# Slots for the recurrent unit's gates at the write, longer planned latencies, and down-product weights prepared one step ahead

## The chip, the core and the metric

The kernel runs on one core of a Trainium2 chip. The core's engines are TensorE (PE, with its weight loads as PEld), VectorE (DVE), ScalarE (ACT), GpSimd (POOL) and the queue of SyncE (SP), which issues most DMAs here. The metric is the device time of one execution in microseconds (us), as the median of several runs.

## What is computed

One decoder layer over 512 tokens of width 1024, in float32. All weight products are done as three passes of a split operand (high part times high part, high times low, low times high), so every weight tile has to be split into two tiles before its product.

```
proj = x @ w_in                                   # q k v z, b a, lru_x lru_g, gate_dn gate_lru
o    = gated_delta_rule(l2norm(silu(conv(q,k,v))), g, beta)   # 8 heads, scan over chunks
y_dn = (rmsnorm(o) * silu(z)) @ w_branch_dn
u    = conv(lru_x) + b
r, i = sigmoid(u @ w_a + b_a), sigmoid(u @ w_i + b_i)         # 10 blocks of 128
a    = exp(-8 r softplus(-lambda));  h = scan(a, sqrt(1 - a^2) * i * u)
y_lru = (h * gelu(lru_g)) @ w_branch_lru
h1   = layer_norm(alpha * x + (sig(g_dn) * y_dn + sig(g_lru) * y_lru) @ w_out)
out  = layer_norm(alpha * h1 + (silu(h1 @ w_gate) * (h1 @ w_up)) @ w_down)
```

## The kernel before

**Order of the work.** PE's instructions run in the order in which the program emits them. The other engines' instructions are put in order at compile time by a scheduler that goes by priority (program order, lifted inside `urgent()`) and by its own model of when data is ready; so an instruction late in the program can be placed long before its place there, if its data is ready and its engine has nothing earlier to do.

**First half (to about 500 us).** A planner writes PE's order. `before_merge` goes through the jobs of `ORDER` (k, q, v, z projections, l = a pair of recurrent blocks, g = merge gates) and takes the first whose number of free slots in `NEED` is there; each job is two columns of 8 steps, and `play` fetches columns two ahead. A step of a projection adds 0.68 to the planner's `clock`. Beside them run *chains*, generators that emit a few small matmuls, then yield how long PE was used and a planned latency from the table `LAT`; a chain is taken up again when the planner's clock has passed its due time. `dn_chain(p)` is the delta rule for two heads (p = 0 to 3): transposes and norms (`kt`), `kk`, a 16-step substitution on DVE (`sub`), block inverse steps `m1`, `m2`, `i1` to `i5`, then for four chunks `xr` (LAT `su`), `su` (LAT `ks`), `ks` (LAT `xr`), at last `oa`, `ob` and, 26 later, `ot`. `until(f"s{p-1}")` lets chain p begin its substitution only when chain p-1 is past `m2`. If no job fits, the planner adds 0.68 to its clock and goes on with the chains alone.

**Slots.** 40 SBUF slots of 128 x 1024 float32 are handed out in the order in which they came free. `slot()` takes one when the program text reaches it, `free()` gives it back; `room(n)` lets a chain wait, in planner time, for n free slots. `lru_pair(p)` takes three at its start (u, r, ig), though r and ig are first written in `lru_chain`, and `lru_chain` takes a and gl after its matmuls; the gelu that writes gl waits in planner time for that (`while p not in gls`).

**Feed-forward and down product.** After `play(ffn())` the down product is done as seven products q = 0 to 6 (a11, s1, s2, a12, s4, s3, a22), each in six steps m (five of two blocks of 256 rows, one of one). The sums s1 to s4 and the combined weights `td` make seven products of eight. A step loads its weights (`load_w`, three buffers), splits them with an ACT copy for the high part and a DVE subtract for the low part (`split_w`, three buffers each), and runs 12 matmuls of 512 columns. In the last product ("final") steps 3 to 5 have slots of their own and are run in one go, first for row block 2, then for row block 3. Results are added to the rows by `Norm.add` on DVE; `p7_done` does two such adds for each of row blocks 2 and 3 after s3. `Norm.finish` normalises: for row blocks 0 and 1 with ACT and four POOL instructions each, for 2 and 3 on DVE.

```
        for m, (p, n) in enumerate(blocks):
            keep = final and m >= 3
            extra = [flat(slot(f"wd{m}{e}", F32R)) if keep else None for e in range(2)]
            pend.append((m, n, *split_w(load_w(right(p, n)), None, *extra)))
            if not final:
                ready.append(left(products[q + 1][0], p, n))
```

So a step's weights are emitted right before its matmuls, and behind the adds of the step before. The last product's first accumulator `dl0` is the next bank of ring p, which is the one that s3 accumulated in for row block 2.

Of the kernel before, what the change touches and what calls it, by code (L numbers as in the profile page):

```python
# [9 lines left out]
F32R = mybir.dt.float32r  # L10
I32 = mybir.dt.int32
AF = mybir.ActivationFunctionType
# [8 lines left out]
         "z1 l3 v3 q3 g0 z2 g1 l4 g2 g3 z3 g4 g5 g6 g7")  # L21

LAT = {
    "F": 13.0, "kt": 12.0, "q": 5.2, "qk": 5.0, "P": 4.0, "vt": 2.0, "u": 10.0, "sub": 33.0, "m1": 7.0,
    "m2": 8.0, "i2": 6.0, "i4": 7.0, "i5": 7.0, "x": 8.0, "ks": 5.0, "xr": 7.0, "su": 6.5, "ot": 26.0,
    "ba": 9.0, "g": 2.5, "conv": 14.0,
}

# [5 lines left out]
P = 128  # L34
# [12 lines left out]
def layer_kernel(  # L47
# [23 lines left out]
    def slot(name, dt=F32):  # L71
        if not line:
            raise RuntimeError(f"no slot for {name}")
        tag = line.pop(0)
        t = big.tile([P, 2, T], dt, tag=tag, name=name)
        held[id(t)] = (t, tag)
        return t
# [12 lines left out]
    def bankp(name):  # L90
        return bank("p", name)

    def bankd(name):
        return bank("d", name)
# [19 lines left out]
    def flat(t):  # L114
        return t.rearrange("p a b -> p (a b)")
# [10 lines left out]
    def act(o, i, func, **kw):  # L126
        return S.activation(out=o, in_=i, func=func, **kw)  # L127
# [36 lines left out]
    def load_w(src, raw=None):  # L164

        wcount[0] += 1
        if raw is None:
            raw = wp.tile([P, 1024], F32, tag="wr", bufs=3, name=f"wr{wcount[0]}")
        v = view_w(raw, *src.shape[1:])
        nc.sync.dma_start(out=v, in_=src)  # L170
        return v

    def split_w(raw, eng=None, hi=None, lo=None):

        wcount[0] += 1
        if hi is None:
            hi = wp.tile([P, 1024], F32R, tag="wh", name=f"wh{wcount[0]}")
        if lo is None:
            lo = wp.tile([P, 1024], F32R, tag="wl", name=f"wl{wcount[0]}")
        n = raw.shape[1] * raw.shape[2]  # L180
        split_flat(hi[:, :n], lo[:, :n], raw.rearrange("p a b -> p (a b)"), eng)
        return view_w(hi, *raw.shape[1:]), view_w(lo, *raw.shape[1:])
# [80 lines left out]
    with tc.manual_schedule(engines={mybir.EngineType.Activation, mybir.EngineType.DVE}):  # L263
        for k in range(NK):
            transpose_x(k)
            if k == 1:
                n = NK * 16
# [20 lines left out]
    clock = [0.0]  # L288

    def advance(flush=False):  # L290
        while flush and chains:
            clock[0] += 0.68
            advance()
        for ch in list(chains):
            while ch in chains and ch[0] <= clock[0]:
                try:
                    pe, lat = next(ch[1])
                    ch[0] = clock[0] + pe + lat
                    clock[0] += pe
                except StopIteration:  # L300
                    chains.remove(ch)
# [19 lines left out]
    def start(gen, lat):  # L321
        chains.append([clock[0] + lat, gen])
# [113 lines left out]
    def room(n):  # L436
        while len(line) < n:
            assert clock[0] < 2000.0
            yield 0.0, 0.65
# [327 lines left out]
        yield 0.9, 0.0  # L767


    hs, gls = [None] * 5, {}  # L770

    def lru_pair(p):
        n0 = 2 * p
        u, r, ig = slot(f"u{p}"), slot(f"r{p}"), slot(f"ig{p}")
        gw = wg.tile([P, 4, P], F32, tag="gr" if p % 2 else "gs", name=f"gr{p}")
        nc.sync.dma_start(out=gw[:, 0:2], in_=lru_w_a[0, n0:n0 + 2].rearrange("n i o -> i n o"))
        nc.sync.dma_start(out=gw[:, 2:4], in_=lru_w_i[0, n0:n0 + 2].rearrange("n i o -> i n o"))

        def then_u(j, ps):
            conv(u[:, j], ps, lru_w, n0 + j, bias=lru_p(0, n0 + j))  # L780
            if j == 1:
                start(lru_chain(p, u, r, ig, gw), LAT["u"])

        keep = []

        def then_g(j, ps):
            keep.append(ps)
            if j == 1:
                while p not in gls:
                    clock[0] += 0.68  # L790
                    advance()
                with urgent():
                    for i in range(2):
                        act(gls[p][:, i], keep[i], AF.Gelu_apprx_tanh)
                done[f"gl{p}"] = clock[0]

        c = CLX + 256 * p
        yield from columns(win[:, :, c:c + 256], xT, f"lx{p}", then_u, G)
        c = CLG + 256 * p
        yield from columns(win[:, :, c:c + 256], xT, f"lg{p}", then_g, G)  # L800

    def lru_chain(p, u, r, ig, gw):
        n0 = 2 * p
        for g, (t, b) in enumerate(((r, 1), (ig, 2))):
            for j in range(2):
                ps = bankd(f"lw{p}_{g}_{j}")
                PE.matmul(ps, gw[:, 2 * g + j], u[:, j], start=True, stop=True)
                act(t[:, j], ps, AF.Sigmoid, bias=lru_p(b, n0 + j))
                if g == 0 or j == 0:
                    yield 0.86, PIECE  # L810
        if p == 0:
            lru_rates()
        a, gl = slot(f"a{p}"), slot(f"gl{p}")
        gls[p] = gl
        tt(V, u, u, ig, ALU.mult)
        m = ig
        for j in range(2):
            act(a[:, j], r[:, j], AF.Exp, scale=c8n[:, n0 + j:n0 + j + 1])
            act(r[:, j], r[:, j], AF.Tanh, scale=c8[:, n0 + j:n0 + j + 1])
        act(m, a, AF.Square)  # L820
        stt(m, m, 1.0, r, ALU.add, ALU.mult)
        act(m, m, AF.Sqrt, bias=tiny)
        V.memset(m[:, :, 0:1], 1.0)
        tt(V, m, m, u, ALU.mult)
        yield 0.86, 0.0
        yield from until(f"gl{p}")
        h = u
        for j in range(2):
            V.tensor_tensor_scan(out=h[:, j], data0=a[:, j], data1=m[:, j], initial=0.0,
                                 op0=ALU.mult, op1=ALU.add)  # L830
        tt(V, h, h, gl, ALU.mult)
        free(r, a, gl, ig)
        hs[p] = h
# [37 lines left out]
    for n in range(4 * NK):  # L871

        k, i = (n // 4, n % 4) if n < 24 else (6 + n % 2, (n - 24) // 2)
# [151 lines left out]
    for i in range(4):  # L1025
        t = slot(f"h1{i}")
# [49 lines left out]
    wgt, wup, wd = rows(w_ffn_gate[0]), rows(w_ffn_up[0]), rows(w_ffn_down[0])  # L1076
    NP = NF // 2
    parts = {n: [] for n in ("a12", "a22", "s1", "s2", "s3", "s4")}
    a11 = []
# [94 lines left out]
    def left(n, p, m):  # L1174

        t = slot(f"{n}{p}", F32R)
        split(t[:, 0, 0:256 * m], t[:, 1, 0:256 * m], flat(parts[n][p // 4])[:, 256 * (p % 4):256 * (p % 4 + m)])
        if p % 4 == 2 or p + m == NP:
            free(parts[n][p // 4])
        return t  # L1180
# [20 lines left out]
        ("s3", combined(1), ca, False, p7_done),  # L1201
        ("a22", combined(2), [], True, None),
    ]
    ready = a11
    for q, (name, right, banks, new, then) in enumerate(products):
        lhs, ready = ready, []
        final = q == 6
        tops = [[(0, b)] for b in banks]
        if final:

            tops = [[(0, bankp("dl0"))], [(0, bankd("dl1")[:, 0:256]), (256, bankd("dl2")[:, 0:256])]]
        pend = []
        for m, (p, n) in enumerate(blocks):
            keep = final and m >= 3
            extra = [flat(slot(f"wd{m}{e}", F32R)) if keep else None for e in range(2)]
            pend.append((m, n, *split_w(load_w(right(p, n)), None, *extra)))
            if not final:
                ready.append(left(products[q + 1][0], p, n))
            if keep and m < 5:
                continue  # L1220
            last = m == len(blocks) - 1
            for i in range(2):
                for c, ps in tops[i]:
                    w = ps.shape[1]
                    for mm, nn, wh, wl in pend:
                        for k in range(nn):
                            ts = slice(256 * k + P * i, 256 * k + P * i + P)
                            mm3(ps, lhs[mm][:, 0, ts], lhs[mm][:, 1, ts], wh[:, k, c:c + w], wl[:, k, c:c + w],
                                new and mm == k == 0, last and mm == m and k == nn - 1,
                                **({} if new else dict(skip_group_check=True)))  # L1230
                    if last:
                        if final:
                            lns[2 + i].add(ps, c, 1.0)
                        else:
                            then(i, ps)
                if last and (final or name == "s4"):
                    t = i if name == "s4" else 2 + i
                    lns[t].finish(final)
                    for jj in range(2):
                        (nc.sync if final else G).dma_start(out=out[0, t * P:(t + 1) * P, T * jj:T * jj + T],  # L1240
                                                            in_=h1[t][:, jj])
            pend = []
        free(*lhs)
# [24 lines left out]
```

## Time and profile before

| what | us |
|---|---|
| median of 3 runs | 1019.58 (1019.29 to 1020.12) |
| profiled execution, its own time | 1017.21 |
| its span, first to last instruction | 1015.5 |
| PE busy | 985.5 (97%) |
| DVE busy | 621.8 (61%) |
| ACT busy | 451.3 (44%) |
| POOL busy | 268.7 (26%) |
| mean granted TensorE clock | 0.995 |

The busy shares are means over stages of different kinds, and PE does the same matmuls whatever waits it meets: what an edit of order can give is read from PE's idle time, stage by stage. A PE row of the timeline gives in brackets the idle time just before it and what ended it. The clock column is the granted TensorE clock as a share of full speed.

### The profile page before, as it was taken

To read this page: it belongs to the slowest core of one execution; us is meant where nothing else is said; L and a number is where in the kernel's file an instruction comes from. 1 tells how busy PE (TensorE), PEld (TensorE's weight loads), DVE (VectorE), ACT (ScalarE), POOL (GpSimd) and SP (SyncE) were. 2 spreads that over 40 slices of the span, in tenths; PEclk is the share of its full clock that TensorE was granted. 3 is DMA by queue.
4 is the path that set the end of the run, shared out by engine and by line. 5 is a ranking of instruction groups with operands and counts; after the bars stand their busy time and mean duration, and the time that the engine had idled before them with its cause. 6 is when DMAs were issued, how large, how long until landed. Compare 5 with 4: busy or idle time off the path is not lost.

```text
span 1015.5 us, 14361 instructions
## 1 busy us (share of the span) xinstructions
PE 985.5 (97%) x5531; PEld 810.5 (80%) x5531; DVE 621.8 (61%) x1318; ACT 451.3 (44%) x619; POOL 268.7 (26%) x278
## 2 busy tenths in 40 slices
PE   7999999999999999999999999999999999999986
PEld 4887767777887888788888888798888888888875
DVE  3678999846777791265223464976344443388676
ACT  4598365359416743574322234322222222375451
POOL 2473534425343724265200003132000100000041
PEclk9999999999999999999999999999999999999998
DMA  8331322323222223234332527579354563346653
GB/s 255 105 104 53 84 74 63 84 73 84 64 63 73 75 66 89 63 112 127 103 94 84 171 88 207 187 268 327 110 163 154 181 207 90 97 136 195 194 188 107
DMA packets 161288, 128.52 MB, mean 127 GB/s; under 512 B 5499, under 2 KB 140860, under 8 KB 161220
## 3 DMA queue, kind: packets, MB, share of 16 engines
q1 hardware_dynamic: 152032, 99.12, 33.3%
q0 software_dynamic: 7872, 28.32, 7.5%
q8 instruction: 43, 0.70, 0.3%
q10 hardware_dynamic: 1316, 0.16, 0.1%
q14 instruction: 25, 0.20, 0.1%
HBM read 113.94 MB, written 13.65 MB: 126 GB/s over the span
## 4 chain that ended last, share of the span: by engine, by line
PE 75%; DVE 14%; ACT 4%; POOL 2%; issue 2%; DMA 1%; ACTq 0%; DVEq 0%; POOLq 0%
PE fu L157 4%; PE fg L157 4%; PE fg L155 4%; PE fu L155 4%; PE fu L156 4%; PE fg L156 4%; PE pj L155 3%; PE pj L156 3%; PE pj L157 3%; PE g L155 3%; PE g L157 3%; PE g L156 3%; DVE xa L121 3%; PE yl L157 2%; PE yl L156 2%
## 5 line engine op out<-in xcount | busy, mean ns | idle before, releaser
L135 ACT CAST wh<-wr 128x1024 fp32r<-128x1024 f32 (+1 forms) x163 | 168.5, 1034 | 363.2 <-PE fg L156 74.3
L121 POOL TENSOR_TENSOR wl<-wr,wh 128x512 fp32r<-128x512 f32 x128 | 172.4, 1369 | 216.0 <-ACT wh L135 211.5
L121 DVE TENSOR_TENSOR wl<-wr,wh 128x1024 fp32r<-128x1024 f32 x99 | 120.1, 1215 | 113.0 <-ACT wh L135 112.9
L155 PE MATMUL pj<-xT,wh 128*128 128x512 f32 x224 | 91.9, 410 | 0.0
L157 PE MATMUL pj<-xT,wl 128*128 128x512 f32 x224 | 87.5, 391 | 0.0
L156 PE MATMUL pj<-xT,wh 128*128 128x512 f32 x224 | 87.4, 390 | 0.0
L127 ACT ACT_TABLE_LOAD x62 | 79.5, 1283 | 12.4 <-DMA rw<-in_lru_conv_w 6.9
L155 PE MATMUL fg<-hk,wh 128*128 128x512 f32 x160 | 62.3, 389 | 0.0
L156 PE MATMUL fg<-hk,wh 128*128 128x512 f32 x160 | 62.3, 389 | 0.0
L157 PE MATMUL fg<-hk,wl 128*128 128x512 f32 x160 | 62.2, 389 | 0.0
L155 PE MATMUL fu<-hk,wh 128*128 128x512 f32 x160 | 62.2, 389 | 0.0
L156 PE MATMUL fu<-hk,wh 128*128 128x512 f32 x160 | 62.2, 389 | 0.0
L157 PE MATMUL fu<-hk,wl 128*128 128x512 f32 x160 | 62.2, 389 | 0.0
L155 PE MATMUL g<-xT,wh 128*128 128x512 f32 x128 | 51.1, 399 | 0.0
L157 PE MATMUL g<-xT,wl 128*128 128x512 f32 x128 | 50.0, 391 | 0.0
L156 PE MATMUL g<-xT,wh 128*128 128x512 f32 x128 | 49.9, 390 | 0.0
L124 DVE SCALAR_TENSOR_TENSOR x<-pj,cols,x 128x511 f32<-128x511 f32 (+2 forms) x60 | 44.5, 742 | 8.6 <-ACT x L127 8.2
L157 PEld LDWEIGHTS pj<-xT,wl 128*128 128x128 f32 x224 | 42.0, 188 | 9.1
L155 PEld LDWEIGHTS pj<-xT,wh 128*128 128x128 f32 x224 | 42.1, 188 | 7.9
L121 POOL TENSOR_TENSOR h<-h,g 128x512 f32<-128x512 f32 x4 | 6.0, 1499 | 160.2 <-ACT h L127 160.2
L156 PEld LDWEIGHTS pj<-xT,wh 128*128 128x128 f32 x224 | 42.2, 188 | 7.1
L121 DVE TENSOR_TENSOR xa<-xa 128x16 f32<-128x16 f32 (+14 forms) x116 | 37.6, 324 | 2.3
(387 smaller groups left out, 2366.2 us busy)
## 6 DMA issues: line engine op xcount, KB each, us to landing
wr<-in_w_in SPq DMA_DIRECT2D x64, 512.0 KB, 3.6
wr<-in_w_ffn_gate SPq DMA_DIRECT2D x22, 512.0 KB, 3.7
wr<-in_w_ffn_up SPq DMA_DIRECT2D x22, 512.0 KB, 3.7
b<-in_w_ffn_down POOLq DMA_DIRECT2D x22, 512.0 KB, 5.2
td<-b POOLq DMA_DIRECT2D x22, 512.0 KB, 4.0
wr<-td SPq DMA_DIRECT2D x20, 512.0 KB, 3.7
wr<-in_w_ffn_down SPq DMA_DIRECT2D x15, 512.0 KB, 3.4
wr<-in_w_branch_lru SPq DMA_DIRECT2D x8, 512.0 KB, 3.4
```

The source lines that it names most:

```text
L121: return eng.tensor_tensor(out=o, in0=a, in1=b, op=op)
L124: return V.scalar_tensor_tensor(out=o, in0=a, scalar=s, in1=b, op0=op0, op1=op1)
L127: return S.activation(out=o, in_=i, func=func, **kw)
L135: S.copy(out=hi, in_=src)
L155: PE.matmul(ps, wh, rh, start=start, stop=False, **kw)
L156: PE.matmul(ps, wh, rl, start=False, stop=False, **kw)
L157: PE.matmul(ps, wl, rh, start=False, stop=stop, **kw)
```

## The change

1. `lru_pair` takes u and gl; `lru_chain` first waits for three free slots and then takes r, ig and a. The gelu no longer waits in planner time.
2. Twelve entries of `LAT` grow, by 0.5 to 1.5 each; `sub`, `u`, `ot`, `F`, `q`, `vt`, `ba`, `g` and `conv` stay.
3. In the down products `prepare(q, m)` loads and splits a step's weights (and makes the left operand of the next product) before the matmuls of the step ahead of it, across the border between two products too.
4. The last product's `dl0` is `cc[0]`, the bank that a12 used, in place of the next of the ring.
5. `finish` and the output DMAs of row blocks 0 and 1 are emitted after s3's adds and no longer after s4's.

```diff
--- before.py
+++ after.py
@@ -21,8 +21,8 @@
          "z1 l3 v3 q3 g0 z2 g1 l4 g2 g3 z3 g4 g5 g6 g7")
 
 LAT = {
-    "F": 13.0, "kt": 12.0, "q": 5.2, "qk": 5.0, "P": 4.0, "vt": 2.0, "u": 10.0, "sub": 33.0, "m1": 7.0,
-    "m2": 8.0, "i2": 6.0, "i4": 7.0, "i5": 7.0, "x": 8.0, "ks": 5.0, "xr": 7.0, "su": 6.5, "ot": 26.0,
+    "F": 13.0, "kt": 13.5, "q": 5.2, "qk": 5.5, "P": 4.5, "vt": 2.0, "u": 10.0, "sub": 33.0, "m1": 8.5,
+    "m2": 9.5, "i2": 7.0, "i4": 7.5, "i5": 7.5, "x": 8.5, "ks": 6.0, "xr": 7.5, "su": 7.0, "ot": 26.0,
     "ba": 9.0, "g": 2.5, "conv": 14.0,
 }
 
@@ -767,11 +767,11 @@
         yield 0.9, 0.0
 
 
-    hs, gls = [None] * 5, {}
+    hs = [None] * 5
 
     def lru_pair(p):
         n0 = 2 * p
-        u, r, ig = slot(f"u{p}"), slot(f"r{p}"), slot(f"ig{p}")
+        u, gl = slot(f"u{p}"), slot(f"gl{p}")
         gw = wg.tile([P, 4, P], F32, tag="gr" if p % 2 else "gs", name=f"gr{p}")
         nc.sync.dma_start(out=gw[:, 0:2], in_=lru_w_a[0, n0:n0 + 2].rearrange("n i o -> i n o"))
         nc.sync.dma_start(out=gw[:, 2:4], in_=lru_w_i[0, n0:n0 + 2].rearrange("n i o -> i n o"))
@@ -779,19 +779,16 @@
         def then_u(j, ps):
             conv(u[:, j], ps, lru_w, n0 + j, bias=lru_p(0, n0 + j))
             if j == 1:
-                start(lru_chain(p, u, r, ig, gw), LAT["u"])
+                start(lru_chain(p, u, gl, gw), LAT["u"])
 
         keep = []
 
         def then_g(j, ps):
             keep.append(ps)
             if j == 1:
-                while p not in gls:
-                    clock[0] += 0.68
-                    advance()
                 with urgent():
                     for i in range(2):
-                        act(gls[p][:, i], keep[i], AF.Gelu_apprx_tanh)
+                        act(gl[:, i], keep[i], AF.Gelu_apprx_tanh)
                 done[f"gl{p}"] = clock[0]
 
         c = CLX + 256 * p
@@ -799,8 +796,10 @@
         c = CLG + 256 * p
         yield from columns(win[:, :, c:c + 256], xT, f"lg{p}", then_g, G)
 
-    def lru_chain(p, u, r, ig, gw):
+    def lru_chain(p, u, gl, gw):
         n0 = 2 * p
+        yield from room(3)
+        r, ig, a = slot(f"r{p}"), slot(f"ig{p}"), slot(f"a{p}")
         for g, (t, b) in enumerate(((r, 1), (ig, 2))):
             for j in range(2):
                 ps = bankd(f"lw{p}_{g}_{j}")
@@ -810,8 +809,6 @@
                     yield 0.86, PIECE
         if p == 0:
             lru_rates()
-        a, gl = slot(f"a{p}"), slot(f"gl{p}")
-        gls[p] = gl
         tt(V, u, u, ig, ALU.mult)
         m = ig
         for j in range(2):
@@ -1201,22 +1198,32 @@
         ("s3", combined(1), ca, False, p7_done),
         ("a22", combined(2), [], True, None),
     ]
-    ready = a11
+    lefts, steps = [a11] + [[] for _ in products], {}
+
+    def prepare(q, m):
+
+        p, n = blocks[m]
+        own = q == 6 and m >= 3
+        extra = [flat(slot(f"wd{m}{e}", F32R)) if own else None for e in range(2)]
+        steps[q, m] = (m, n, *split_w(load_w(products[q][1](p, n)), None, *extra))
+        if q < 6:
+            lefts[q + 1].append(left(products[q + 1][0], p, n))
+
+    todo = [(q, m) for q in range(7) for m in range(len(blocks))]
+    prepare(*todo.pop(0))
     for q, (name, right, banks, new, then) in enumerate(products):
-        lhs, ready = ready, []
+        lhs = lefts[q]
         final = q == 6
         tops = [[(0, b)] for b in banks]
         if final:
 
-            tops = [[(0, bankp("dl0"))], [(0, bankd("dl1")[:, 0:256]), (256, bankd("dl2")[:, 0:256])]]
+            tops = [[(0, cc[0])], [(0, bankd("dl1")[:, 0:256]), (256, bankd("dl2")[:, 0:256])]]
         pend = []
-        for m, (p, n) in enumerate(blocks):
-            keep = final and m >= 3
-            extra = [flat(slot(f"wd{m}{e}", F32R)) if keep else None for e in range(2)]
-            pend.append((m, n, *split_w(load_w(right(p, n)), None, *extra)))
-            if not final:
-                ready.append(left(products[q + 1][0], p, n))
-            if keep and m < 5:
+        for m in range(len(blocks)):
+            if todo:
+                prepare(*todo.pop(0))
+            pend.append(steps.pop((q, m)))
+            if final and 3 <= m < 5:
                 continue
             last = m == len(blocks) - 1
             for i in range(2):
@@ -1233,8 +1240,8 @@
                             lns[2 + i].add(ps, c, 1.0)
                         else:
                             then(i, ps)
-                if last and (final or name == "s4"):
-                    t = i if name == "s4" else 2 + i
+                if last and (final or name == "s3"):
+                    t = 2 + i if final else i
                     lns[t].finish(final)
                     for jj in range(2):
                         (nc.sync if final else G).dma_start(out=out[0, t * P:(t + 1) * P, T * jj:T * jj + T],
```

## Rows read from the trace of the kernel before

**Rows 1.** Busy by stretch: us; PE, PEld, DVE, ACT, POOL (instructions); clock; DMA share, GB/s.

```profile
100.00:150.00 50.00, 46.52 (x415) 35.77 (x414) 47.34 (x148) 26.54 (x34) 24.43 (x29) 0.97 0.31 84
150.00:200.00 50.00, 48.09 (x434) 38.72 (x432) 45.35 (x109) 22.78 (x30) 23.27 (x24) 1.00 0.26 70
200.00:350.00 150.00, 146.74 (x1100) 120.18 (x1099) 104.61 (x274) 85.89 (x107) 64.14 (x59) 1.00 0.25 69
...
896.90:986.80 89.90, 89.90 (x397) 74.14 (x395) 69.31 (x100) 53.59 (x73) 7.46 (x6) 1.00 0.58 184
986.80:1006.30 19.50, 15.99 (x100) 14.13 (x99) 14.30 (x25) 3.87 (x5) 6.12 (x7) 1.00 0.34 110
1006.30:1015.50 9.20, 0.00 (x0) 0.00 (x0) 6.10 (x17) 0.20 (x1) 0.00 (x0) 0.63 0.29 114
```

**Rows 2.** Timeline of PE, the instructions that waited between 50 and 500 us.

```profile
117.29 0.44 PE L633 MATMUL m<-xa 32*32 32x16 f32 x32 [1.55 <-DVE Fl L124]
...
137.78 0.21 PE L669 MATMUL i<-xa 32*32 32x32 f32 x1 [0.86 <-DVE xa L664]
...
144.42 0.79 PE L542 MATMUL kk<-x 128*128 128x128 f32 x5 [0.99 <-DVE rkb L121]
...
178.30 0.28 PE L633 MATMUL m<-xa 32*32 32x16 f32 x11 [0.62 <-DVE xa L627]
...
182.18 0.38 PE L708 MATMUL ks<-Fl,x 128*128 128x128 f32 x1 [1.28 <-DVE Fl L725]
...
248.88 0.28 PE L660 MATMUL i<-xa,Fl 32*32 32x32 f32 x7 [1.99 <-DVE vb L121]
...
320.05 0.38 PE L708 MATMUL ks<-Fl,x 128*128 128x128 f32 x1 [1.26 <-DVE Fl L124]
```

**Rows 3.** Timeline of PE and DVE, what the wait at 320 us waited for.

```profile
312.73 0.27 PE L722 MATMUL su<-xa,kd 128*128 128x128 f32 x1
...
319.66 0.34 DVE L124 SCALAR_TENSOR_TENSOR Fl<-Fl,egl,su 128x128 f32<-128x128 f32 x1
```

**Rows 4.** Busy time by stretch, one us after the wait at 117 us.

```profile
119.00:120.00 1.00, 1.00 (x34) 0.84 (x34) 1.00 (x2) 0.00 (x0) 0.94 (x3) 0.50 0.00 0
```

**Rows 5.** Timeline of PE after that wait, first slow and first fast projection matmul.

```profile
117.66 0.68 PE L155 MATMUL lx<-xT,wh 128*128 128x512 f32 x1
...
121.12 0.45 PE L155 MATMUL lx<-xT,wh 128*128 128x512 f32 x1
```

**Rows 6.** Timeline of PE, the two waits in the last down product.

```profile
989.52 0.47 PE L155 MATMUL dl<-wh,a 128*128 128x512 f32 x1 [2.69 <-DVE h L124]
...
993.55 0.50 PE L156 MATMUL dl<-wl,a 128*128 128x512 f32 x1 [0.76 <-DVE wl L121]
```

**Rows 7.** Timeline of DVE, from a split of s3's weights to the last product's.

```profile
978.48 1.22 DVE L121 TENSOR_TENSOR wl<-wr,wh 128x1024 fp32r<-128x1024 f32 x1 [0.19 <-ACT wh L135]
...
984.77 3.40 DVE L121 TENSOR_TENSOR wl<-wr,wh 128x1024 fp32r<-128x1024 f32 x1 [1.93 <-ACT wh L135]
988.10 1.27 DVE L124 SCALAR_TENSOR_TENSOR h<-h,da 128x512 f32<-128x512 f32 x2
...
991.21 0.73 DVE L124 SCALAR_TENSOR_TENSOR h<-h,da 128x256 f32<-128x256 f32 x2
991.86 2.77 DVE L121 TENSOR_TENSOR wl<-wr,wh 128x1024 fp32r<-128x1024 f32 x2
```

**Rows 8.** Timeline of POOL, normalisation of row blocks 0 and 1.

```profile
979.24 1.61 POOL L121 TENSOR_TENSOR h<-h,g 128x512 f32<-128x512 f32 x1 [160.23 <-ACT h L127]
...
984.55 1.30 POOL L121 TENSOR_TENSOR h<-h,b 128x512 f32<-128x512 f32 x1
985.80 1.28 POOL L121 TENSOR_TENSOR h<-h,g 128x512 f32<-128x512 f32 x1
...
991.10 1.30 POOL L121 TENSOR_TENSOR h<-h,b 128x512 f32<-128x512 f32 x1
```

**Rows 9.** Timeline of ACT, the copy for the last product's second step.

```profile
985.55 1.05 ACT L135 CAST wh<-wr 128x1024 fp32r<-128x1024 f32 x1 [0.81 <-PE da L157]
```

## Prediction

> **What bounds the kernel now.** I read the busy times first, then PE's waits in order of time, then DVE and POOL around each wait. PE is busy for 985.5 of 1015.5 us, and none of the edits adds or removes a matmul. So the gain can only come from PE's idle time, and the busy times by stretch say where it lies: 3.48, 1.91 and 3.26 us in the three stretches from 100 to 350 us, nothing in the 89.9 us of the first six down products, 3.51 us in the last product, and the 9.2 us tail in which DVE normalises the last rows alone [rows 1]. The start-up and the border to the feed-forward part hold the rest, and no edit reaches them.
>
> From 100 to 350 us the reader should see that every wait is a small matmul of a delta-rule chain held up by DVE: seven waits, 1.55 + 0.86 + 0.99 + 0.62 + 1.28 + 1.99 + 1.26 = 8.55 us [rows 2]. PE stands in the emitted order, so the projection matmuls behind the waiting one can't fill the hole. DVE is 47.3 and 45.4 us busy in the 50 us stretches where five of the seven lie [rows 1], so a chain's result comes late because DVE has other work queued in front. The wait at 320 shows it: the `su` matmul ran at 312.73, but DVE got to its result only at 319.66, and `ks` had been placed before that [rows 3].
>
> The first wait costs more than its 1.55 us. Behind it the granted clock is 0.50 of full speed, the 1.2 GHz level [rows 4]. From 117.66 to 121.12 PE ran six projection matmuls and the second half of `m2` [rows 5]. At full speed a 512-column matmul takes 89.90 / 396 = 0.227 us (six products of 66) [rows 1], and the first half of `m2` took 117.66 - 117.29 = 0.37 us [rows 2, 5]. That makes 6 x 0.227 + 0.37 = 1.73 us where 3.46 passed, so 1.7 us were lost to the clock, after the idle time and 32 tiny matmuls.
>
> In the last product PE waits 2.69 us for `dl0`'s bank, which DVE still reads for s3, and 0.76 us for a low part [rows 6].
>
> **Longer latencies.** Nothing is added to any engine: PE's order alone changes, a chain's step standing one or two projection steps (0.68 each) further back. Taking each wait less the growth of the table entry ahead of it: `m1` +1.5 leaves 0.05 of 1.55 and nothing of 0.62; `i2` +1.0 ends the 0.86; `kt` +1.5 ends the 0.99; `ks` +1.0 leaves 0.28 of 1.28 and 0.26 of 1.26; `m2` +1.5 leaves 0.49 of 1.99. Together 1.08 of 8.55 remain, so 7.47 us go. If the 1.55 goes, so should the 1.7 us of half clock: 9.2 us at best. What hides the moved step is the projection work put in its place, which PE has to do anyway. If that cover is gone (no job fits), the idle time returns.
>
> I don't take all of it. DVE's order is made anew with the new emission order, the chains shift against each other (chain 0 by 13.5 us over its whole length, below), and DVE has only 2.7 and 4.7 us left in the two fullest stretches [rows 1]. Some step that is now in time will be late. The bounds are 0 (the waits only move) and 9.2; new waits of about 2.7 us, two or three of the mean size 8.55 / 7 = 1.2, leave **-6.5 us**.
>
> Do longer chains cost anything at the end? Chain 0 takes kt, m1, m2 (4.5), i2 to x (2.5) and its four chunks (6.5): 13.5 us more. Chains 1 and 2 add another 3 each, since their substitution waits for `m2` of the one before: 16.5 and 19.5. The last transposes of chain 3 are needed only at the first branch product of the delta rule, behind the 80 steps of the recurrent branch product, three matmuls or 0.68 us each, 54 us. Its own 13.5 us disappear there.
>
> **Slots.** A pair holds two slots and not three while its four columns run, and five from the chain's start to its end, as before. No instruction is added. Does the wait for three free slots, or the longer chains, stop the planner? At its tightest, when z0 is placed, the old order holds 8 tiles of x, 8 for each of chains 0 to 2 (k, q, F, Fl, kd, xa, vb, Yf), 3 for chain 3 (k, F, Fl), 3 recurrent results and z0: 39 of 40. Following the clock through the code, chain 0 then gives back 2 slots at planner time 208.9 and 5 more at 211.1, and z1 asks for 2 at 225.0. With 13.5 more, the releases fall to 222.4 and 224.6: 2.6 before z1 asks. The recurrent chain of pair 2 finds 5 free where it needs 3. So it fits, narrowly, and I cost this edit at **0**; what covers it are those 2.6 of planner time. Gelu's wait in planner time goes with it; it happened at two pairs, for a step or two.
>
> **Steps prepared ahead.** In the first six products PE has no idle time [rows 1], so a step further ahead gives nothing there: splits already ran as far ahead as three buffers allow. DVE, ACT and the SP queue issue the same instructions in nearly the same order, since they are placed by readiness; the copy for the second step of the last product already starts at 985.55, before s3 ends [rows 9]. **0**.
>
> **`dl0` on another bank, and the last product.** The 2.69 us wait for the bank goes. What is late next is the low part of the second step. DVE is one queue here: the first step's split 984.77 to 988.17, s3's adds and statistics 988.10 to 991.94, then two splits in 2.77 us [rows 7]; PE took up the second step at 993.55 [rows 6]. Starting the first step 2.69 us earlier only lengthens the wait after it, unless DVE is earlier too. It can be: the first split took 3.40 us where the same shape took 1.22 at 978.48 [rows 7], while POOL was at its instructions from 984.55 on [rows 8]. Without this delay s3's adds, which can start 0.68 us (three matmuls) before s3's last matmul at 986.8, so at 986.2, take their 3.8 us to 990.0, and the next split 1.2 to 991.2: at most 993.5 - 991.2 = 2.3 us earlier. Were the splits put ahead of the adds, both waits could go: 3.45 us.
>
> The Trainium skill (SBUF — State Buffer, section Who interferes with whom) says that a VectorE instruction with two SBUF inputs contends with a GpSimd instruction that reads SBUF, and that whoever comes second is blocked for the whole instruction. The 3.40 us split against 1.22 agrees. By the page alone this part would gain nothing while row blocks 0 and 1 are normalised at this time.
>
> **`finish` after s3.** Its data are ready once s4's adds are done, and a late place only makes it yield to s3's splits; I expect POOL's eight instructions to stay within a few us of 979.24 to 992.4 [rows 8]. Bounds for the last product as a whole: all 3.45 us gained, or, if POOL's work moves behind s3, two more splits on PE's path blocked as the one was, 2 x (3.40 - 1.22) = 4.4 us lost. Nearest is the row of before, with one blocked split: **-1.0 us**.
>
> **Sum.** 1017.21 (the profiled execution's own time) - 6.5 - 1.0 = 1009.7; the median of the runs shown is 2.4 us above that execution, so **1012.1 us**.
>
> **Rivals.** *The waits only move.* DVE is nearly full from 100 to 200 us, and more projection steps before a chain step also bring their convolutions, which have priority on DVE. Then a chain's result is as late as before: 1019.58 - 1.0 = 1018.6 us. For it: the DVE rows; against it: DVE has 45 us free from 200 to 350 [rows 1], where two of the waits lie. *The planner runs out of slots* (the slower one): between z0 and z1 chain 0 slips past its due times and z1 finds fewer than two slots. The planner then passes time with chain steps alone, and PE has nothing between them. Each 0.68 of such time is a projection step not there; it ends above the old time once it passes 7.5 us, and measurably once it passes 9.5, that is if chain 0 slips 9.5 + 2.6 = 12.1 us beyond the 13.5, as much again. One such stop of 10 us gives 1022. *POOL's work lands in the last product.* The page's rule as a mechanism here: +4.4 in place of -1.0 gives 1017.5, with the first half's gain. For it: the emission place; against it: placement by readiness. *The change does nothing*: PE is 97% busy, and the waits are hidden elsewhere; PE's waits are on its own order, so I give it no part apart from the first rival.
>
> **How the numbers follow.** The measurement tells about 0.2% (2 us) from no change. Forecast 0.62, all faster; waits only move 0.24, of which 0.06 faster by a partial gain, 0.15 the same and 0.03 slower; POOL 0.06, on the edge, same; slots 0.08, slower. Faster 0.68, same 0.21, slower 0.11. The forecast's own range is 1008.5 (all 9.2 and 2.3 gained would be 1008.1) to 1016. For 8 in 10 I take 1008.0 to 1019.5: it takes in the first rival and POOL's, and leaves out the slots.
>
> **What would show it.** Right: the waits of PE between 100 and 350 us sum to about 2 to 3.5 us; no stretch at half clock near 117; `dl`'s first matmul right behind s3's last, then a wait of 1 to 4 us for a low part; no idle in the first six products. Wrong: chain waits that still sum to 8 us; chain matmuls standing next to each other without projections between 220 and 260 us; splits of 2 us and more in the last product, with POOL's eight instructions beside them.

## The result and the profile after

The kernel after takes 1026.51 us (median of 4 runs, 1025.72 to 1028.10), the kernel before 1019.43 us (4 runs, 1017.72 to 1020.12) beside it: a ratio of 1.0074, 95% interval 1.0055 to 1.0092. So it is 7 us slower where 7 us faster had been forecast, and lies outside the forecast's 1008.0 to 1019.5.

The busy times by stretch of the kernel after, with the same columns as [rows 1]; the last three stretches are again the first six down products, the last product and the tail; the first two of these start 7.6 us later than before, the tail 8.2:

```profile
100.00:150.00 50.00, 42.51 (x377) 32.06 (x376) 48.47 (x139) 23.93 (x30) 25.53 (x27) 0.93 0.28 75
150.00:200.00 50.00, 50.00 (x414) 41.00 (x413) 44.15 (x111) 26.09 (x34) 24.66 (x26) 1.00 0.26 70
200.00:350.00 150.00, 143.29 (x1112) 116.85 (x1111) 101.34 (x274) 82.19 (x103) 59.72 (x59) 0.98 0.26 71
904.50:994.40 89.90, 89.90 (x398) 74.45 (x397) 67.80 (x101) 53.50 (x73) 5.16 (x5) 1.00 0.57 183
994.40:1014.50 20.10, 16.81 (x100) 14.92 (x98) 14.77 (x23) 3.98 (x5) 7.94 (x8) 0.92 0.33 112
1014.50:1024.00 9.50, 0.24 (x3) 0.04 (x1) 6.40 (x18) 0.20 (x1) 0.00 (x0) 0.65 0.29 110
```

The reader should see three things. PE's idle time from 100 to 350 us is 7.49 + 0 + 6.71 = 14.20 us, against 3.48 + 1.91 + 3.26 = 8.65 us before [rows 1]. The granted clock fell too, from 0.97 to 0.93 in the first stretch and from 1.00 to 0.98 in the third. And the last product takes about 0.9 us longer: its last `dl` matmul starts at 1014.5 instead of 1006.0, 8.5 us later, of which 7.6 came from earlier. The first branch product of the recurrent unit begins at 514.9 instead of 507.8 us, so nearly the whole loss is made before that point: 5.55 us of the 7.1 is added idle time, which leaves at most 1.5 us for the lower clock. These are readings of one execution each. The kernels with the slots alone and with the down products alone, below, have the old table and still show 0.93 from 100 to 150 us in their profiles, so the 0.97 before is not what the old table always gives.

PE's waits in the same part, which answer to [rows 2]:

```profile
119.48 0.44 PE L633 MATMUL m<-xa 32*32 32x16 f32 x32 [1.17 <-DVE Fl L124]
...
131.93 0.44 PE L660 MATMUL i<-xa,Fl 32*32 32x32 f32 x17 [0.80 <-DVE xa L121]
...
142.65 1.19 PE L806 MATMUL lw<-u,gr 128*128 128x512 f32 x1 [5.52 <-DVE u L124]
...
207.79 0.41 PE L485 MATMUL vt<-ident,x 128*128 128x128 f32 x2 [0.69 <-DVE F L121]
...
263.23 0.80 PE L559 MATMUL qk<-x,x 128*128 128x128 f32 x5 [2.24 <-DVE rq L142]
...
312.40 1.01 PE L708 MATMUL ks<-Fl,x 128*128 128x128 f32 x3 [3.61 <-DVE Fl L725]
```

With one of 0.18 us that is not shown these are seven again, 14.2 us. After the two longest the clock stands at the lower level, 1.2 GHz, for some microseconds: it reads 0.50 from 142 to 146 and from 312 to 317 us. The means over six microseconds (busy time by stretch, from 142 and from 312 us):

```profile
142.00:148.00 6.00, 5.35 (x13) 2.90 (x13) 5.94 (x34) 3.21 (x4) 0.00 (x0) 0.59 0.00 1
...
312.00:318.00 6.00, 5.60 (x18) 4.73 (x19) 5.86 (x17) 0.00 (x0) 0.00 (x0) 0.54 0.33 89
```

Six of the seven old waits are gone, and the one at `m` is 1.17 us instead of 1.55. The 3.61 us at 312 us is new: it is the first `ks` step of the third chain, which waits for a copy (L725) and did not wait before (it ran at 297.75 us). The step that waited at 320 us before is that chain's second, which now runs at 339.50 us without a wait. The largest new wait stands at a matmul that no latency was changed for, the gate matmul `lw`, whose entry `u` stayed at 10. It waits for the convolution of `u`. ScalarE had finished the input of that convolution at 127.00 + 0.78 = 127.8 us; DVE came to it at 139.26. DVE's queue in between (timeline of DVE, columns start, length, engine, line):

```profile
124.12 0.18 DVE L121 TENSOR_TENSOR xa<-xa 128x8 f32<-128x8 f32 x1
...
125.88 2.28 DVE L121 TENSOR_TENSOR xa<-xa 128x32 f32<-128x32 f32 x2
...
133.06 0.61 DVE L121 TENSOR_TENSOR xa<-xa 128x64 f32<-128x64 f32 x2
...
134.01 2.28 DVE L121 TENSOR_TENSOR xa<-xa 128x72 f32<-128x72 f32 x2
136.33 0.01 DVE L600 LOAD_MASK_SELECT xa<-xa  x1
136.33 0.26 DVE L600 STREAM_SHUFFLE xa<-xa 128x80 f32<-128x80 f32 x1
136.63 2.13 DVE L121 TENSOR_TENSOR xa<-xa 128x80 f32<-128x80 f32 x2
...
139.26 0.74 DVE L124 SCALAR_TENSOR_TENSOR u<-lx,cols,u 128x511 f32<-128x511 f32 x1
```

and POOL at the same times (timeline of POOL):

```profile
125.57 2.54 POOL L121 TENSOR_TENSOR wl<-wr,wh 128x512 fp32r<-128x512 f32 x2 [1.16 <-ACT wh L135]
...
133.68 4.99 POOL L121 TENSOR_TENSOR wl<-wr,wh 128x512 fp32r<-128x512 f32 x4
```

A pair of these small substitution instructions takes 0.61 us when POOL is not subtracting, and 2.1 to 2.3 us when it is: three such pairs lose about 3 x 1.6 = 4.9 us, close to the 5.52 us that PE waits. Ahead of the 3.61 us wait stand two more such pairs (timelines of DVE and POOL):

```profile
302.05 2.52 POOL L121 TENSOR_TENSOR wl<-wr,wh 128x512 fp32r<-128x512 f32 x2 [3.37 <-ACT wh L135]
302.11 2.54 DVE L121 TENSOR_TENSOR xa<-xa 128x64 f32<-128x64 f32 x2
...
308.42 2.51 POOL L121 TENSOR_TENSOR wl<-wr,wh 128x512 fp32r<-128x512 f32 x2 [2.95 <-ACT wh L135]
308.50 2.56 DVE L121 TENSOR_TENSOR xa<-xa 128x104 f32<-128x104 f32 x2
```

That is a reading; the runs below test it.

In the last product the bank is free at once, but DVE and POOL meet again (timeline of POOL, DVE and PE, which answers to [rows 6 to 8]):

```profile
989.14 1.29 POOL L121 TENSOR_TENSOR h<-h,g 128x512 f32<-128x512 f32 x1 [162.20 <-ACT h L127]
...
992.14 1.99 DVE L121 TENSOR_TENSOR wl<-wr,wh 128x1024 fp32r<-128x1024 f32 x1 [3.08 <-ACT wh L135]
...
997.82 5.09 DVE L121 TENSOR_TENSOR wl<-wr,wh 128x1024 fp32r<-128x1024 f32 x2
...
1000.13 1.69 POOL L121 TENSOR_TENSOR h<-h,b 128x512 f32<-128x512 f32 x1
...
1000.74 0.80 PE L156 MATMUL dc<-wl,a 128*128 128x512 f32 x1 [3.29 <-DVE wl L121]
1001.34 0.63 PE L157 MATMUL dc<-wh,a 128*128 128x512 f32 x1
```

POOL's normalisation of row blocks 0 and 1 starts 10 us later than before, but 7.6 of these come from the first half: measured from the start of s3's last matmul (994.05, before 986.44) it starts 4.9 us ahead where it was 7.2 us ahead. These 2.3 us are enough to move the harm from the first split (1.99 us instead of 3.40) to the two splits behind it, which PE waits for (5.09 us instead of 2.77) [rows 7]. The three take 7.08 us together where they took 6.17. PE waits 3.29 us for the first of the two, and runs at half clock for about three microseconds behind it (0.63 us a matmul; granted clock 0.50 from 1000.7 to 1003.6 us).

### The profile page after: what moved, and what is told of

Read it like the earlier page. It is cut to its first block, busy times and chain, and to the rows that moved or that the text cites. A ratio compares the mean times of both kernels' runs of the same rounds, so it can differ in the third digit from the quotient of the medians.

```text
span 1024.0 us, 14359 instructions
## 1 busy us (share of the span) xinstructions
PE 987.7 (96%) x5531; PEld 813.1 (79%) x5531; DVE 620.1 (61%) x1318; ACT 451.2 (44%) x619; POOL 268.4 (26%) x278
## 4 chain that ended last, share of the span: by engine, by line
PE 73%; DVE 17%; ACT 3%; issue 2%; DMA 2%; POOL 2%; DVEq 0%; SPq 0%; POOLq 0%; ACTq 0%
DVE xa L121 4%; PE fg L156 4%; PE fu L156 4%; PE fg L157 4%; PE fu L157 4%; PE fg L155 4%; PE fu L155 4%; PE pj L155 3%; PE g L155 3%; PE g L157 3%; PE g L156 3%; PE pj L156 3%; PE pj L157 3%; DVE x L124 2%; PE yl L157 2%
## 5 line engine op out<-in xcount | busy, mean ns | idle before, releaser
L121 POOL TENSOR_TENSOR wl<-wr,wh 128x512 fp32r<-128x512 f32 x128 | 175.3, 1392 | 226.4 <-ACT wh L135 225.9
L121 DVE TENSOR_TENSOR xa<-xa 128x16 f32<-128x16 f32 (+14 forms) x116 | 45.6, 393 | 2.9
```

The costliest lines, as they stand in the source:

```text
L121: return eng.tensor_tensor(out=o, in0=a, in1=b, op=op)
```

## The experiments

Two theories at first. *Latencies*: the longer table entries by themselves make the first half slower, by a new order of DVE's work. *Planner*: the slot edit makes the planner stop and wait. Later a third, which the readings above suggest. *Reads*: what makes a chain late is that POOL's subtracts block DVE's two-operand instructions, and the table entries only decide which chain is hit. Ratios are against the kernel before, timed in the same batch (1018.1 to 1018.8 us), and a gain or loss in us with a ratio is that share of it.

**One part of the change at a time.** Three kernels: before with the new table alone; before with the slot edit alone; before with the edits of the down products alone.

```diff
-    "F": 13.0, "kt": 12.0, "q": 5.2, "qk": 5.0, "P": 4.0, "vt": 2.0, "u": 10.0, "sub": 33.0, "m1": 7.0,
+    "F": 13.0, "kt": 13.5, "q": 5.2, "qk": 5.5, "P": 4.5, "vt": 2.0, "u": 10.0, "sub": 33.0, "m1": 8.5,
...
```

> The kernel before with the longer latencies alone. The changed kernel lost 7.6 us ahead of the down products, in seven waits of PE on DVE between 110 and 320 us (14.2 us against 8.55 before) and about 2 us of half clock behind them. If the longer latencies do that by making DVE's order anew, this kernel is 5 to 9 us slower than before, with PE waits of 10 us or more between 100 and 350 us. If the slots of the recurrent unit do it, it is 3 to 9 us faster, as was forecast for this part.

> The kernel before with the recurrent unit's slots alone. If this edit only moves the moment at which a slot is taken, the time stays within 2 us of before and the seven waits stay near 8.5 us in sum. If it is what put the 5.52 us wait of the recurrent unit's second gate matmul there, that wait is here too and the kernel is 4 to 8 us slower.

> The kernel before with the three edits of the down products alone. The changed kernel lost 0.9 us from the end of s3 to the last matmul: the bank wait of 2.69 us is gone, but a wait of 3.3 us for a low part and half clock behind it came. If that is this part's own doing, the time is 0.5 to 2 us above before, with the first half as before. If the down products only suffered from being reached at another time, it is 1 to 3 us faster, as forecast.

Measured: the table alone 1027.66 us (ratio 1.0085, 1.0070 to 1.0100, so 8.7 us lost); the slots alone 1019.12 (1.0000, 0.9990 to 1.0009); the down products alone 1019.56 (1.0012, 1.0001 to 1.0023, 1.2 us lost). The table alone brings the waits of the kernel after one by one, for instance (timeline of PE, table alone):

```profile
142.67 2.05 PE L807 MATMUL lw<-u,gr 128*128 128x512 f32 x2 [5.51 <-DVE u L124]
```

So the loss is the table's, the slots are worth nothing, and the last product loses about a microsecond on its own; in the profiled execution it is 2.3: from s3's last matmul (987.5) to the last `dl` matmul (1009.4) it takes 21.9 us, before 19.6 (986.4 to 1006.0). With the slots alone the waits stand at the same seven matmuls, but sum to 9.6 us: the one at `m` is 3.05 us there.

**`finish` put back to s4 in the kernel after.**

```diff
-                if last and (final or name == "s3"):
+                if last and (final or name == "s4"):
```

> The changed kernel with the normalisation of row blocks 0 and 1 put back behind s4's adds. If POOL's eight instructions, which ran from 989 to 1002 us and not from 979 to 992, blocked the splits of the last product (5.09 us for two, where 2.4 are normal), they now run 8 to 10 us earlier, the two splits take less than 3.5 us, and the last product ends 2 to 4 us earlier than in the changed kernel. If the place of that work doesn't matter, the time stays within 1 us of the changed kernel.

Measured: 1025.94 us (1.0070, 1.0055 to 1.0086). POOL's work starts 7.2 us ahead of s3's last matmul again, so it was the later `finish` that had moved it. The two splits take 2.78 us, as expected; but the last product, 19.6 us as before and without half clock, is only 0.8 us shorter than in the kernel after, not 2 to 4, and the time stays within 1 us of that kernel's. The free bank gives nothing: POOL's work is back beside the first split (3.41 us), PE waits 1.18 and 2.24 us for low parts instead of 2.69 for the bank and 0.76 [rows 6]. DVE's chain bounds this product, not the bank alone.

**A longer latency for the wait that appeared**, `u` from 10 to 16 in the kernel after.

```diff
-    ... "vt": 2.0, "u": 10.0, "sub": 33.0, ...
+    ... "vt": 2.0, "u": 16.0, "sub": 33.0, ...
```

> The changed kernel with the planned latency of the recurrent gates' input (u) at 16 and not 10. In the changed kernel the second gate matmul waits 5.5 us for a convolution that DVE reached late. If the wait is there because that one entry was left at 10 while the delta-rule chains around it moved back, it goes, no other wait of its size takes its place, and the kernel is 5 to 8 us faster than the changed one, so within 3 us of the kernel before. If waits only change places whenever PE's order changes, the sum of PE's waits from 100 to 350 us stays above 10 us and the gain is under 3 us.

Measured: 1023.67 us (1.0047, 1.0031 to 1.0063). The 5.5 us wait goes, and others come: 2.26 at `i`, 2.40 at a projection that waits for `u`, 4.17 at `qt`, which waits for ScalarE; 9.9 us in all, just under the 10 of the second case, whose small gain (under 3 us) came. The substitution instructions of DVE, 45.6 us in the kernel after (shown below), take 39.4 us here, near the 37.6 of the kernel before, and yet the kernel is 0.47% slower than before: not all that a table costs is this stretching.

**Half of each longer latency**, in the kernel before.

```diff
-    ... "kt": 12.0, ... "m1": 7.0,
+    ... "kt": 12.75, ... "m1": 7.75,
```

> The kernel before with half of each growth of the latencies. If longer latencies cost time in proportion to their length, it is 3 to 6 us slower than before. If each new order of PE simply draws other waits, the time may fall on either side, between 4 us faster and 10 us slower, with waits at other places than both kernels'.

Measured: 1021.1 us (1.0026, 1.0017 to 1.0036), 2.7 us slower, at the edge of the first case and inside the second; the sum of waits is 11.5 us, with a 4.91 us wait at the same `lw` as in the kernel after and a new one of 2.23 us at 319 us. So each new table draws another set of waits; none of the three longer tables tried draws less than 8.55 us.

**POOL writes instead of reading.** In the kernel before and in the kernel after POOL writes zeros where it had subtracted. The low parts of the weights of those projections, and of the first four feed-forward columns, are left out by this; the matmuls are all there.

```diff
-            tt(eng or V, lo[:, c:c + step], src[:, c:c + step], f(hi[:, c:c + step]), ALU.subtract)
+            G.memset(f(lo[:, c:c + step]), 0.0) if eng is G else tt(V, ...)
```

> The kernel before, with the low parts that GpSimd makes in the projections and the first feed-forward pair left out: GpSimd writes zeros there and reads nothing. PE's order is the same, DVE has the same instructions in nearly the same order. If GpSimd's two-operand instructions block DVE and so make the chains late, the seven waits (8.55 us) shrink to under 4 us and DVE's small two-operand instructions lose their durations of over 1 us. If DVE is late from its own queue of work, the waits stay within 2 us of 8.55.

> The changed kernel with the same low parts left out. If GpSimd's blocking of DVE is what made the changed kernel's waits 14.2 us, they shrink to under 5 us here, and the 8 us between the two kernels shrink to under 3 us. If the new order is bad by itself, 5 us or more of the difference stay, with the 5.5 and 3.6 us waits still there.

Measured: 1004.77 us from before (0.9862, 0.9845 to 0.9878) and 1004.51 us from after (0.9858, 0.9844 to 0.9873). Both lose their waits (1.79 us and 0.88 us are left between 100 and 350), and they are equal: without the reads the whole change, the longer table with it, costs nothing, nor does it gain. A write also need not wait for ScalarE's high part; but none of PE's waits between 100 and 350 us, before or after, was for a low part made by POOL. The same stretch of DVE in the second of them (timeline of DVE):

```profile
118.83 0.17 DVE L121 TENSOR_TENSOR xa<-xa 128x8 f32<-128x8 f32 x1
...
126.90 0.51 DVE L121 TENSOR_TENSOR xa<-xa 128x72 f32<-128x72 f32 x2
...
127.75 0.52 DVE L121 TENSOR_TENSOR xa<-xa 128x80 f32<-128x80 f32 x2
...
129.06 0.74 DVE L124 SCALAR_TENSOR_TENSOR u<-lx,cols,u 128x511 f32<-128x511 f32 x1
```

The pairs of 2.28 and 2.13 us take 0.51 and 0.52. The convolution of `u` comes 10 us earlier; half of that is from before this stretch, and from the first substitution instruction to the convolution it takes 10.2 us instead of 15.1, which are the 4.9 us that the three pairs lost.

But POOL was also done sooner: a write takes 0.53 us, a subtract 1.37. **POOL writes three times** tells the two apart (same part left out, in the kernel before):

```diff
+            for _ in range(3 if eng is G else 1):
+                if eng is G:
+                    G.memset(f(lo[:, c:c + step]), 0.0)
```

> The kernel before, with POOL's two subtracts per projection column replaced by three writes of zero over each 512-column half (the low parts of those weights, the second and third term of those products, are left out). POOL is then busy longer than with the subtracts (by the single write's 0.53 us, an estimate of 3 x 0.53 = 1.6 us per half against 1.37 us) but reads nothing. If it is POOL's reads that hold up VectorE's small two-operand instructions: about 1005 us, as with one write (1004.8), the longest substitution instruction still under 0.5 us. If it was POOL's shorter work that gained the 14 us: 1015 to 1025 us, with matrix-product waits of 8 us or more between 100 and 350 us.

Measured: 1006.46 us (0.9878, 0.9859 to 0.9897). POOL is 118.8 us busy between 100 and 350 us, more than before's 111.9, and DVE is still hardly held up (the longest substitution instruction took 0.81 us, over the 0.5 expected, but their mean is 0.24). The group of substitution instructions by line, in the kernel before, after, and with three writes (busy us, mean ns of one, idle before):

```profile
L121 DVE TENSOR_TENSOR xa<-xa 128x16 f32<-128x16 f32 (+14 forms) x116 | 37.6, 324 | 2.3
```

```profile
L121 DVE TENSOR_TENSOR xa<-xa 128x16 f32<-128x16 f32 (+14 forms) x116 | 45.6, 393 | 2.9
```

```profile
L121 DVE TENSOR_TENSOR xa<-xa 128x16 f32<-128x16 f32 (+14 forms) x116 | 27.8, 239 | 2.3
```

Of the 14 us that one write saves, 12 are still saved, and these are not POOL's shorter work; the 1.7 us between one write and three may be POOL's time, or in part the difference of two timings. With one write, 10 of the 14 us are saved ahead of the first branch product (497.6 us instead of 507.8).

**The reads moved to DVE, nothing left out.** The kernel after with the projections' low parts on DVE; the same with `finish` at s4 on DVE and ScalarE alone; and that one with the old table.

```diff
-            yield from columns(win[:, :, c:c + 256], xT, f"pj{col}_{p}", then, G)
+            yield from columns(win[:, :, c:c + 256], xT, f"pj{col}_{p}", then)
...
-                if last and (final or name == "s3"):
+                if last and (final or name == "s4"):
...
-                    lns[t].finish(final)
+                    lns[t].finish(True)
```

> The kernel after, with the low parts of the projection columns subtracted by VectorE (one 128x1024 instruction, 1.22 us where it stood alone in the trace of before) instead of POOL (two of 1.37 us); nothing left out. If holding up by POOL's reads is what costs: the substitution's instructions shrink to under 0.5 us, the added VectorE work (about 20 columns x 1.22 = 24 us between 100 and 350 us) is in part paid by what is no longer blocked (15 us), the waits of 14.2 us fall below 8, and the time is 1008 to 1016 us. If VectorE's fill at 100 to 200 us (94%) is the tighter limit: the waits stay above 12 us and the time is 1020 us or more.

> As the kernel with the columns on VectorE, and the normalisation of the first two row blocks done after s4 (as before) and by VectorE and ScalarE alone, so that POOL does nothing beside the last products; nothing left out. If POOL's two scalings beside the splits cost the last product its wait and its half clock: no split there over 1.5 us, the last product 18 to 19 us instead of 20.5 us, and the time 1.0 to 2.5 us below that of the columns on VectorE. If VectorE's chain of adds bounds it anyway: within 0.7 us of it.

> As the kernel with columns and normalisation on VectorE, but with the latencies of the kernel before. If the longer latencies cost time only through POOL's reads: within 3 us of the kernel with the longer ones, on either side. If the longer latencies cost time by themselves (about 7 us): 5 to 9 us faster than it.

Measured: 1016.39 us (0.9980, 0.9970 to 0.9989) with the columns on DVE, 1012.67 us (0.9939, 0.9922 to 0.9956) with `finish` moved as well, and 1017.57 us (0.9987, 0.9971 to 1.0002) with the old table. The first lies just above its 1008 to 1016 us, with waits of 7.1 us as expected. The second beats both kernels, by 6 us the one before; it gains 3.7 us on the first, more than the 1.0 to 2.5 expected, and its last product takes 17.3 us where the first has 21.7 (splits of 5.08 us for two, and half clock). DVE's substitution falls to 26.8 us. DVE as a whole has 207.7 us to do from 100 to 350 us instead of 194.0 in the kernel after, and PE still waits half as long: so it was not the amount of DVE's work alone that made the 14.2 us. What is left there is two waits (timeline of PE, the one with `finish` moved):

```profile
110.04 0.80 PE L157 MATMUL pj<-xT,wl 128*128 128x512 f32 x1 [5.53 <-DVE wl L121]
```

The other is 1.63 us at `qk`. This one is the price of the move: the split now stands in DVE's queue behind the recurrent chain's long instructions. The splits of the last product, with POOL at rest (timelines of DVE and PE, same kernel):

```profile
988.43 2.35 DVE L121 TENSOR_TENSOR wl<-wr,wh 128x1024 fp32r<-128x1024 f32 x2
...
989.70 0.50 PE L156 MATMUL dc<-wl,a 128*128 128x512 f32 x1 [1.42 <-DVE wl L121]
```

Two splits in 2.35 us instead of 5.09; from s3's last matmul (984.87) to the last `dl` matmul (1002.12) it takes 17.3 us, 3.2 less than in the kernel after (994.05 to 1014.47) and 2.3 less than before. Whether the free bank has a part in that, no run tells.

The last expectation fell: the old table is 4.9 us slower than the new one here, more than the 3 us that *reads* allowed, though not in the direction of *latencies*. Its waits sum to 3.14 + 2.84 + 3.25 = 9.2 us against 7.2, and its clock is 0.86 against 0.93 from 100 to 150 us; but that profile is of an execution of 1021.48 us, the longest of ten that begin at 1012.76, within the range of the new table's. So why the old table takes longer here is not shown. And chains are late here without a POOL subtract beside them, so the reads are not the only cause of a wait. The table's effect has either sign, by the waits that it draws: +8.7 us (0.85%) beside POOL's subtracts, nothing where POOL writes instead, -4.9 with the splits on DVE.

## Why the prediction was wrong, by its steps

- **Longer latencies, -6.5 us: the step that failed; it measured +8.7 us alone and +7.6 in the changed kernel's profile.** The subtraction itself was not the error: six of the seven old waits went. Wrong was the allowance for new ones, 2.7 us by counting two or three of the mean size, where 14.2 us stood in the end. The text had DVE with 2.7 and 4.7 us left in the two fullest stretches (95% and 91% busy) and said that some step would be late; it took the size of the new wait from the old waits, not from what is queued ahead on DVE. That the table does it is shown by the table alone; half the table and `u` at 16 show that other tables draw other waits.
- **What made DVE late was put down to "other work queued in front".** Part of it was not work: the substitution's 37.6 us are 26.8 to 27.8 where POOL only writes, 10 us less, and the 45.6 of the kernel after are 28.3. The prediction cites the rule that says so, the Trainium skill (SBUF — State Buffer, section Who interferes with whom), for one split in the last product; the substitution meets it far more often, on instructions that last a fifth of POOL's. The runs agree with it: 0.51 us for a pair beside writes, 2.1 to 2.3 beside subtracts.
- **The half clock, 1.7 us back: wrong in sum.** Behind the wait at `m`, now 1.17 us, the clock is 1.00, as forecast; but it is 0.93 in that stretch, since it fell in the wait of 5.52 us before 142 us instead. The 1.7 us were also read from one execution: with the down products alone, the 1.56 us wait at `m` has full clock behind it.
- **Slots, 0: right** (ratio 1.0000). The slower rival, a planner without slots, did not occur.
- **Steps prepared ahead, 0: right**; the first six products still take 89.90 us without idle time. The edit had no run of its own.
- **`dl0` and `finish`, -1.0 us: wrong, +0.9 us in the profile and 1.2 us alone.** Two steps failed. The text had POOL's eight instructions stay within a few us of their place, and they did: against s3 they moved 2.3 us back. Wrong was that this would leave one blocked split, as before; it frees the first in part and blocks the two that PE waits for (5.09 against 2.77 us). That is the rival *POOL's work lands in the last product*: the two splits lose 2.3 us together where it gave 4.4, and the product 0.9 us on balance. And the bank was not worth its 2.69 us: with `finish` back, this product takes 19.6 us as before.
- **Rivals.** *The waits only move* named the mechanism that came, DVE's full queue, but its price ended at zero gain; nothing in it made the new waits longer than the old.

What stays open is which table would be best beside POOL's subtracts; four were tried, counting the old one, and the old one is the fastest. How much of the loss is idle time and how much is clock is told only by the profiles, not by a run of its own. That POOL's reads are needed for the loss is shown by the kernels without them; that each single wait of the kernel after is their doing is read from the rows for the waits of 5.52 and 3.61 us alone.

## What to carry to other kernels

A wait on an in-order engine that is 95% full may only change its place when it is planned for, as here: its length comes from what stands ahead on that queue, so look there first and ask whether those instructions take their own time or are held up by another engine. Compare one instruction's shortest and longest time in the same trace (here 0.14 and 1.33 us for the substitution), and see what the neighbour does during the long ones. Take the neighbour's reads away in one run before tuning any latency; if both versions then come out equal, the latencies cost something only together with those reads. Then look again after the cure: here, with the reads' work on DVE, the same latencies made a difference of 4.9 us, the other way.

## What the runs showed of the hardware

- DVE's small two-operand instructions are stretched to about the length of POOL's, whatever their size: in the kernel before two of 128 x 16 took 2.48 us together at 296 us; in the kernel after the largest, 128 x 120, took up to 1.38 us, and 0.28 us on average with the columns on DVE. POOL's subtract takes 1.37 us on average.
- Beside the same POOL subtracts DVE's one-operand shuffle is not stretched: 56 of them take 13.5 us in the kernel before, in the kernel after and with POOL only writing.
- POOL's writes hardly hold DVE up: 384 writes of 128 x 512 at 0.52 us leave the substitution at 239 ns an instruction, against 231 with a third of the writes.
- The same wait does not always bring the half clock, nor at once. In the kernel before, 0.50 came within 1 us of the 1.55 us wait at `m`; with the down products alone, a 1.56 us wait at the same matmul was followed by 1.00 from 116.7 to 128 us. In the last product of the kernel after, the matmul behind 3.29 us of idle time took 0.80 us and the next ones 0.63. With POOL only writing, the one behind 3.31 us took 0.51 us, the length at full clock, but a microsecond later the clock fell all the same (0.50 from 980.3 to 983.3 us; timeline of PE). No run here tells what decides when.

```profile
979.23 0.51 PE L156 MATMUL dc<-wl,a 128*128 128x512 f32 x1 [3.31 <-DVE wl L121]
...
980.28 0.63 PE L157 MATMUL dc<-wh,a 128*128 128x512 f32 x1
```
